# Squared-ReLU MLP by a seven-product scheme: operand differences made in the first product and kept in DRAM, the norm's factor moved to the second product's sums, the first two pairs of rows interleaved

## The chip, the cores and the metric

The kernel runs on one core of a Trainium2 chip. The metric is the device time of one execution in microseconds (us); lower is better. Of the core's engines, TensorE (PE in the profile) multiplies matrices, and its loading of the stationary operand is shown as PEld. VectorE (DVE), ScalarE (ACT) and GpSimd (POOL) work on tiles elementwise. SyncE (SP) issues most of the DMAs, in order. Each engine takes its own instructions in order, and semaphores join them.

## The reference

The trunk has two residual layers here: neighbourhood attention and an MLP, then a gated DeltaNet and an MLP, with a last norm behind them. SEQ and D_MODEL are 1024, D_FF is 4096, everything is float32. The change touches the two MLPs alone:

```python
def rmsnorm(x, w):
    y = xf * lax.rsqrt(jnp.mean(xf * xf, axis=-1, keepdims=True) + EPS)
    return (y * w.astype(jnp.float32)).astype(x.dtype)

def sq_relu_mlp(h, w1, w2):
    a = jax.nn.relu(h @ w1)
    return (a * a) @ w2

# in the trunk, for each layer:
x = x + mixer(rmsnorm(x, ...))
x = x + sq_relu_mlp(rmsnorm(x, mlp_norm[i]), mlp_w1[i], mlp_w2[i])
```

The mean of squares is one number per token. As the ReLU is taken of something that this positive number only scales, relu(r·u)² is r²·relu(u)², and r² may be multiplied in before or after the second product.

## The kernel before

Activations are kept transposed: 128 channels by 1024 tokens a tile, tokens in two halves of 512. A float32 product is made from a high and a low part of each operand, three matmuls for one (`hi·hi`, `hi·lo`, `lo·hi`). The high part is a copy by ScalarE (`whi` for weights, the left half of a tile for activations), the low part a subtraction by VectorE (`wlo`, the right half; line 242 in `halves`).

Both MLP products use a seven-product (Strassen-Winograd) scheme on 2 x 2 blocks: seven products in the order `ORDER = (1, 5, 2, 6, 3, 7, 4)` take the place of eight. Operands 5, 6, 7 and 4 are sums or differences of blocks. Four blocks of a right side are called 11, 12, 21, 22: the first digit is the even or odd tile of channels, the second the half of the tokens. One product is 12 matmuls of 128 x 512 (four tiles of the inner dimension, three matmuls each), and its result lies in one PSUM bank.

One MLP (`block`) runs in four stages.

1. `out_gather`: the mixer's output product is added to the residual stream `hs`; the sums of squares for the norm are made (`sumsq`), and the operands of the first product are prepared. Preparation that is late is left as functions in `todo`, called at the product that needs them.
2. `mlp_first` (matmuls at line 366): 16 pairs `n` of hidden tiles, seven products each. A pair loads its weights (`quad_weights`, 2 x 512 KB), makes four combinations of them on GpSimd (line 341), and finishes four results of 128 x 512: VectorE does ReLU and the multiplication by `rstd` in one instruction (line 346), ScalarE squares (line 347), and a DMA writes it to `hidden` in DRAM (line 348). In pair 0 the norm is finished between the first products: eight `ones` matmuls sum over the channels (line 194), GpSimd takes the power, eight matmuls spread the factor over the partitions (line 206).
3. `Second.blocks` (matmuls at line 1520): the first three quarters of the inner dimension of the second product, three blocks `b` of 28 products (seven positions, four output rows `q`). `load_b` reads the four blocks of `hidden`; GpSimd makes the four differences of them (`difference`), besides four combinations of weights (`combine`) and some of the sums, all through `less` (line 1359). `split` makes the high and low parts of the next position's operands; weights are split (lines 1513, 1514) in the step that uses them; the sums gather in `h`, `z`, `y`, `w`, of which `h` starts from the residual stream (line 1501).
4. `mlp_second` (matmuls at line 148, sums at line 409): the last quarter, plain, 16 tiles of 24 matmuls; each finished tile goes to `after` (the next norm, or `final_tile`).

The order in which instructions stand on an engine is made at compile time, outside the DeltaNet, by a scheduler that starts from the program's order and moves an instruction ahead where its own timing model says that it is ready. An engine's real order is therefore near the program's order, but not the same.

Of the kernel before, what the change touches and what calls it, by code (L numbers as in the profile page):

```python
# [37 lines left out]
class Trunk:  # L38
# [133 lines left out]
    def sumsq(self, d, half, hv, st):  # L172
        nc = self.nc
        if d == 0:
            st["acc", half] = self.half(f"rs{half}", 1)
# [13 lines left out]
    def rstd_cols(self, st, half, ps=None):  # L189
# [8 lines left out]
        return r  # L198

# [127 lines left out]
    def mlp_first(self, st, w1, get, spare, todo, second, moved):  # L327

        nc = self.nc
        self.hidden = self.dram.tile([w1.shape[1] // P, P, S], FP32, tag="hidden", name=self.uid("hidden"), bufs=1)  # L330
        nq = w1.shape[1] // (2 * P)
        raw = [self.quad_weights(w1, 0)]
        for n in range(nq):
            if n + 1 < nq:
                raw.append(self.quad_weights(w1, n + 1))
            a11, a12, a21, a22 = raw[n]
            own = {i: self.wk2.tile([P, 4, P], FP32, tag=f"s{i}", name=self.uid("s"), bufs=1)
                   for i in ((1, 2, 4, 3) if moved else (3, 1, 2, 4))}
            s1, s2, s3, s4 = [own[i] for i in range(1, 5)]
            for out, x, y, op in ((s1, a21, a22, ALU.add), (s2, s1, a11, ALU.subtract), (s4, a12, s2, ALU.subtract), (s3, a21, a11, ALU.subtract)):  # L340
                nc.gpsimd.tensor_tensor(out=out, in0=x, in1=y, op=op)
            left = {1: a11, 2: a12, 3: s4, 4: a22, 5: s1, 6: s2, 7: s3}
            temp = lambda i: self.slot(f"{spare}{i}", shape=[P, HALF])

            def finish(t, f, half):
                nc.vector.scalar_tensor_tensor(out=t, in0=t, scalar=0.0, in1=st["rstd", half], op0=ALU.max, op1=ALU.mult)  # L346
                nc.scalar.activation(out=t, in_=t, func=AF.Square)  # L347
                nc.sync.dma_start(out=self.hidden[2 * n + f][:, half * HALF:(half + 1) * HALF], in_=t)

            def add(out, x, y, eng=nc.vector):  # L350
                eng.tensor_tensor(out=out, in0=x, in1=y, op=ALU.add)  # L351
                return out

            for j in self.ORDER:
                hi, lo = [self.sb.tile([P, 4, P], F32R, tag=tag, name=self.uid(tag), bufs=3) for tag in ("whi", "wlo")]
                nc.scalar.copy(out=hi, in_=left[j])  # L356
                nc.vector.tensor_tensor(out=lo, in0=left[j], in1=hi.bitcast(FP32), op=ALU.subtract)  # L357
# [3 lines left out]
                pool, tag, bufs = {1: (self.pw, "p1", 1), 5: (self.pw, "p5", 1), 2: (self.ps, "mm", 2), 7: (self.ps, "mm", 2)}.get(j, (self.pw, "pq", 3))  # L361
# [5 lines left out]
                if n == 0 and j == 5:  # L367
                    rcol = [self.rstd_cols(st, half) for half in range(2)]
                if n == 0 and j == 2:
                    for half in range(2):  # L370
                        self.spread(st, half, rcol[half])
# [18 lines left out]
                second.prepare(n - nq, j)  # L390

    def mlp_second(self, a, h, w2, after, tail=2, cut=False):
        nc = self.nc
        w = [None, None]
        for d, half in self.sequence(tail):
            if w[0] != d:
                w = [d, self.weight(w2[w2.shape[0] - D:, d * P:(d + 1) * P])]
            hv = h(d, half)  # L400
            if cut and (d, half) == (ND - 1, 1):
                for part in range(2):
                    sl = slice(part * 256, part * 256 + 256)
                    ps = self.product(w[1], a, half, sl=slice(HALF + sl.start, HALF + sl.stop))
                    nc.vector.tensor_tensor(out=hv[:, sl], in0=ps, in1=hv[:, sl], op=ALU.add)
                    after(d, half, hv[:, sl], part)
                continue
# [908 lines left out]
class Second:  # L1316
# [6 lines left out]
    def __init__(self, tr, group, other, rest, free, w2):  # L1323
# [4 lines left out]
        self.names = {"11": free[4:6], "12": rest[0:2], "21": rest[2:4], "22": rest[4:5] + o(15)}  # L1328
        self.sets = g(0, 8, 1, 9), g(2, 10, 3, 11)
        self.acc = {"z": g(6, 7), "y": g(14, 15)}  # L1330
# [4 lines left out]
    def load_b(self, b, which, i):  # L1335

        nc, tr = self.tr.nc, self.tr
        t = tr.slot(self.names[which][i], shape=[P, 2, HALF])
        f, half = b * ND + 4 * i + int(which[0]) - 1, int(which[1]) - 1
        for k in range(2):  # L1340
            nc.sync.dma_start(out=t[:, k], in_=tr.hidden[f + 2 * k][:, half * HALF:(half + 1) * HALF])
            self.b[which, 2 * i + k] = t[:, k]
# [8 lines left out]
    def split(self, b, pos, i):  # L1351

        j = self.tr.ORDER[pos]
        t = self.tr.slot(self.sets[(7 * b + pos) % 2][i], F32R)
        self.tr.halves(t, self.b[{1: "11", 5: "11", 6: "11", 2: "21", 4: "21", 3: "22", 7: "12"}[j], i])
        self.ops[j, i] = t

    def less(self, out, x, y, op=ALU.subtract):
        self.tr.nc.gpsimd.tensor_tensor(out=out, in0=x, in1=y, op=op)  # L1359

    def difference(self, j, i):

        b = lambda which: self.b[which, i]
        if j == 5:
            self.less(b("11"), b("12"), b("11"))
        elif j == 6:
            self.less(b("11"), b("22"), b("11"))
        elif j == 7:
            self.less(b("12"), b("12"), b("22"))
        else:  # L1370
            self.less(b("21"), b("21"), b("11"))

    def left(self, j, q):
        if j in (5, 6):
            return self.s[q]
        t = self.k[self.block, 1 if j in (1, 7) else 2, q]
        return t[:, :, P:] if j in (7, 4) else t[:, :, :P]

    def combine(self, j, q):

        tr = self.tr
        if j == 5:
            self.s[q] = tr.work("s1", [P, 4, P], 4)
            self.less(self.s[q], self.left(7, q), self.left(4, q), ALU.add)
        elif j == 6:
            self.less(self.s[q], self.s[q], self.left(1, q))
        elif j == 7:
            self.less(self.left(7, q), self.left(7, q), self.left(1, q))
        else:
            self.less(self.left(2, q), self.left(2, q), self.s[q])  # L1390

    def prepare(self, n, j):
# [3 lines left out]
        if n == -3 and j in (1, 2):  # L1396
            self.load_b(0, "11", j - 1)
        if n < -1:
            return
        if j == 1:  # L1400
            for i in range(3):
                self.split(0, 0, i)
            self.load_b(0, "12", 0)
        elif j == 5:
            self.split(0, 0, 3)
            self.load_b(0, "12", 1)
        elif j == 2:
            for i in range(4):
                self.difference(5, i)
            self.load_b(0, "21", 0)  # L1410
            self.load_w(0, 1, 0)
        elif j == 6:
            self.load_b(0, "21", 1)
            for q in range(1, 4):
                self.load_w(0, 1, q)
        elif j == 3:
            for i in range(2):
                self.load_b(0, "22", i)

    def beside(self, b, pos, q):  # L1420

        last = b == self.nb - 1
        if pos < 6:
            self.split(b, pos + 1, q)
        elif not last:
            self.split(b + 1, 0, q)
        if pos == 0:
            self.combine(5, q)
        elif pos == 1:
            self.combine(6, q)  # L1430
            self.difference(6, q)
        elif pos == 2:
            self.difference(7, q)
        elif pos == 3:
            self.combine(3, q)
            self.difference(4, q)
        elif pos == 4:
            self.combine(7, q)
        if not last:
            if pos in (2, 3) and q % 2:  # L1440
                self.load_w(b + 1, 0, 2 * (pos - 2) + q // 2)
            elif pos == 4:
                self.load_b(b + 1, ("11", "22")[q // 2], q % 2)
            elif pos == 5 and q % 2:
                self.load_b(b + 1, "12", q // 2)
            elif pos == 6:
                self.difference(5, q)
                self.load_w(b + 1, 1, q)
                if q % 2:
                    self.load_b(b + 1, "21", q // 2)  # L1450
        else:
            n = 4 * pos + q
# [424 lines left out]
```

## Time and profile before

| what | value |
|---|---|
| median of 3 runs | 2818.93 us (2815.1 to 2823.02) |
| the profiled execution, its own time | 2822.13 us |
| its span, first to last instruction | 2820.3 us |
| mean granted TensorE clock | 0.977 |
| PE, DVE, ACT, POOL busy | 94%, 67%, 43%, 41% |
| DMA, mean | 92 GB/s |
| first MLP: first product, blocks, last quarter | from 605.8, 933.6, 1211.8 us |
| second MLP: first product, blocks, last quarter | from 2090.6, 2426.1, 2704.0 us |

Times in the trace are counted from the span's start. A row of a stretch gives the busy time of each engine and the number of its instructions in brackets, the granted clock as a share of full speed, and the DMA's share and rate. A row of a group gives a duration as least, median and greatest in ns. In a row of the timeline, the bracket at the end is the time that the engine sat idle before it, with what ended that.

### The profile page before, as it was taken

Reading aid. Unit: us, or ns where it says so; the run is one execution under the profiler, and the core shown is the slowest. Engines: PE = TensorE matmul, PEld = TensorE weight load, DVE = VectorE, ACT = ScalarE, POOL = GpSimd, SP = SyncE. Lnnn points to the kernel's source line nnn. Section 1 sums busy time; section 2 is a strip of 40 time slices with the busy share of each in tenths; the row PEclk is TensorE's granted clock in tenths of the full one; section 3 lists DMA queues with packets and bytes.
Section 4 is the critical chain, followed back from the end, with each engine's and each line's share of the span. In section 5 each row is a group of like instructions: output and inputs, shape, how many; then the busy total and the mean of one; then the engine's idle time right before and its main releaser. Section 6 shows DMA issues by size and latency. Waiting matters only on the chain. (4 is left out here: it accounts for less than half of the span.)

```text
span 2820.3 us, 40024 instructions
## 1 busy us (share of the span) xinstructions
PE 2662.4 (94%) x14172; PEld 2086.9 (74%) x14172; DVE 1883.8 (67%) x3381; ACT 1205.2 (43%) x2603; POOL 1169.1 (41%) x1207
## 2 busy tenths in 40 slices
PE   8999999999999889899999999999969999899898
PEld 6766666778888667687787877787858888677677
DVE  5155556665555878854778887887595555878853
ACT  5134444433334444333455555455353333444334
POOL 0111111154444764641344555543164444754741
PEclk9999999999999999999999999999979999999999
DMA  7212212343332623122221122214463332633023
GB/s 194 56 45 48 59 46 53 114 144 122 112 101 93 202 90 105 38 94 79 51 50 46 42 52 51 50 37 125 118 212 114 111 113 94 198 105 105 23 83 115
DMA packets 293430, 260.00 MB, mean 92 GB/s; under 512 B 78319, under 2 KB 230511, under 8 KB 293231
## 3 DMA queue, kind: packets, MB, share of 16 engines
q1 hardware_dynamic: 284814, 248.98, 29.6%
q0 software_dynamic: 3072, 8.39, 1.3%
q8 instruction: 111, 1.82, 0.3%
q10 hardware_dynamic: 5344, 0.09, 0.1%
q14 instruction: 89, 0.72, 0.1%
HBM read 182.52 MB, written 66.49 MB: 88 GB/s over the span
## 5 line engine op out<-in xcount | busy, mean ns | idle before, releaser
L1555 PE MATMUL mm<-A,whi 128*128 128x512 f32 x1216 | 406.2, 415 | 1.1 <-DVE A L1555 1.1
L148 PE MATMUL mm<-X,whi 128*128 128x512 f32 x1024 | 338.7, 403 | 0.7 <-ACT X L657 0.7
L1555 PEld LDWEIGHTS mm<-A,whi 128*128 128x128 f32 x1216 | 216.0, 192 | 41.4 <-DVE A L1555 1.9
L1555 PE MATMUL mm<-A,wlo 128*128 128x512 f32 x608 | 242.1, 398 | 0.0
L148 PEld LDWEIGHTS mm<-X,whi 128*128 128x128 f32 x1024 | 191.1, 189 | 47.4 <-issue 7.5
L148 PE MATMUL mm<-X,wlo 128*128 128x512 f32 x512 | 206.0, 403 | 0.0
L347 ACT ACTIVATE r<-r 128x512 f32<-128x512 f32 x128 | 80.9, 632 | 247.8 <-DVE r L346 245.1
L1555 POOL TENSOR_TENSOR xt<-lp,xi 128x126 f32<-128x126 f32 (+22 forms) x248 | 107.2, 432 | 175.4 <-DMA lp<-dsc 140.2
L357 DVE TENSOR_TENSOR wlo<-s,whi 128x512 fp32r<-128x512 f32 x128 | 121.7, 952 | 82.7 <-ACT whi L356 82.7
L180 POOL TENSOR_TENSOR rs<-rs,r 128x512 f32<-128x512 f32 x55 | 79.4, 1448 | 225.1 <-ACT r L179 225.0
L1555 DVE SCALAR_TENSOR_TENSOR X<-xp,cw,X 128x512 f32<-128x512 f32 x192 | 141.9, 780 | 1.8 <-ACT X L1555 1.1
L1555 PEld LDWEIGHTS mm<-A,wlo 128*128 128x128 f32 x608 | 115.8, 191 | 28.1
L242 DVE TENSOR_TENSOR X<-A,X 128x512 fp32r<-128x512 f32 x93 | 112.4, 1233 | 20.1 <-ACT X L241 19.5
L1555 POOL TENSOR_TENSOR xi<-xi,xt 128x126 f32<-128x126 f32 (+22 forms) x248 | 115.5, 466 | 19.4
L148 PE MATMUL mm<-A,whi 128*128 128x512 f32 (+1 forms) x336 | 109.8, 403 | 12.9 <-DVE hr L304 6.3
L1520 PE MATMUL pq<-X,whi 128*128 128x512 f32 x336 | 110.9, 412 | 10.6 <-ACT whi L1513 10.6
L1520 PE MATMUL pq<-A,whi 128*128 128x512 f32 x336 | 110.0, 409 | 11.5 <-ACT whi L1513 10.6
L598 POOL DMA_DIRECT2D wvraw<-qk x32 | 17.2, 539 | 248.1 <-ACT qk L596 241.5
L346 DVE SCALAR_TENSOR_TENSOR r<-r,rs 128x512 f32<-128x512 f32 x128 | 92.1, 720 | 37.6 <-POOL r L351 37.6
L242 DVE TENSOR_TENSOR A<-X,A 128x512 fp32r<-128x512 f32 x84 | 101.7, 1235 | 20.2 <-ACT A L241 19.6
L128 ACT CAST whi<-wraw 128x512 fp32r<-128x512 f32 (+1 forms) x110 | 66.1, 605 | 108.6 <-PE mm L148 58.2
L148 PEld LDWEIGHTS mm<-X,wlo 128*128 128x128 f32 x512 | 96.6, 189 | 20.8 <-issue 1.7
(396 smaller groups left out, 7245.9 us busy)
## 6 DMA issues: line engine op xcount, KB each, us to landing
quad<-in_mlp_w_dram SPq DMA_DIRECT2D x64, 512.0 KB
hidden<-r SPq DMA_DIRECT2D x128, 256.0 KB
wraw<-in_gdn_w_in_dram SPq DMA_DIRECT2D x64, 256.0 KB
wraw<-in_mlp_w_dram SPq DMA_DIRECT2D x52, 256.0 KB
X<-in_mlp_w_dram SPq DMA_DIRECT2D x24, 512.0 KB
X<-hidden SPq DMA_DIRECT2D x48, 256.0 KB
A<-in_mlp_w_dram SPq DMA_DIRECT2D x24, 512.0 KB
A<-hidden SPq DMA_DIRECT2D x48, 256.0 KB
```

Of the source, the lines that this page charges most:

```text
L128: nc.scalar.copy(out=hi[:, :nk], in_=raw[:, :nk])
L148: nc.tensor.matmul(out=ps, lhsT=a, rhs=b[:, sl], start=n == 0, stop=n == last)
L180: nc.gpsimd.tensor_tensor(out=st["acc", half], in0=st["acc", half], in1=sq, op=ALU.add)
L242: nc.vector.tensor_tensor(out=t[:, HALF:], in0=src, in1=t[:, :HALF].bitcast(FP32), op=ALU.subtract)
L346: nc.vector.scalar_tensor_tensor(out=t, in0=t, scalar=0.0, in1=st["rstd", half], op0=ALU.max, op1=ALU.mult)
L347: nc.scalar.activation(out=t, in_=t, func=AF.Square)
L357: nc.vector.tensor_tensor(out=lo, in0=left[j], in1=hi.bitcast(FP32), op=ALU.subtract)
L598: nc.gpsimd.dma_start(out=ks[i][ab[1 - i], sl].bitcast(FP32), in_=khi[ab[i], sl].bitcast(FP32))
L1520: nc.tensor.matmul(out=ps, lhsT=u[:, i], rhs=x[:, v:v + HALF], start=i == 0 and n == 0, stop=i == 3 and n == 2)
L1555: r = f(*args, **kw)
```

## The change

- In `mlp_first`, ReLU is done by ScalarE without `rstd`; the norm's sums and its spread are no longer made there.
- The four differences of the finished blocks that the second product needs are made there too, on VectorE (`less`), for the first 12 of 16 pairs, and written to a new DRAM tensor `diff`. GpSimd's two additions of a pair become one, VectorE's five from PSUM become six.
- Pairs 0 and 1 take turns for their first four products; pair 0's weight combinations lie in other buffers, `first`.
- In `Second`, an operand set is loaded ready from `hidden` or `diff`, two positions ahead (`load_b`, seven sets of four tiles in a block where there were four); `difference` is gone. Weights are split two products ahead (`split_w`). The residual stream isn't the start of the sums any more, and the copy `r` of product 1 with its addition to `z` is gone.
- `norm_squares` in the middle of the blocks (product 42 of 84) makes 1/(mean of squares) with VectorE's reciprocal and spreads it. In `mlp_second` each tile gets two more VectorE instructions: times this factor, plus the residual stream, which is loaded one tile ahead (`fetch`).
- The sums of squares of the following norm lie in other buffers (`st["at"]`), as the old ones live longer.

```diff
-                self.mlp_first(st, w1, get, other, todo, second, moved)
+                self.mlp_first(w1, get, other, (free[-1], free[0]), todo, second)
...
-            a, h = second.blocks()
-            self.mlp_second(a, h, w2, after, **how)
+            self.mlp_second(second.blocks(st), second.sums, st, w2, after, **how)
...
+    def norm_squares(self, st):
+        nc = self.nc
+        ps = self.bank("pa", [P, HALF])
+        for j in range(8):
+            nc.tensor.matmul(out=ps[:, j:j + 1], lhsT=st["acc", j // 4][:, j % 4 * P:(j % 4 + 1) * P], rhs=self.ones[:, 0:1],
+                             start=True, stop=True)
+        r = self.sb.tile([P, 8], FP32, tag="rcol8", name=self.uid("rcol"), bufs=1)
+        nc.vector.tensor_scalar(out=r, in0=ps[:, 0:8], scalar1=1.0 / D, scalar2=EPS, op0=ALU.mult, op1=ALU.add)
+        nc.vector.reciprocal(out=r, in_=r)
+        for half in range(2):
+            self.spread(st, half, r[:, 4 * half:4 * half + 4])
...
             def finish(t, f, half):
-                nc.vector.scalar_tensor_tensor(out=t, in0=t, scalar=0.0, in1=st["rstd", half], op0=ALU.max, op1=ALU.mult)
+                nc.scalar.activation(out=t, in_=t, func=AF.Relu)
                 nc.scalar.activation(out=t, in_=t, func=AF.Square)
                 nc.sync.dma_start(out=self.hidden[2 * n + f][:, half * HALF:(half + 1) * HALF], in_=t)
+                return t
+
+            def less(i, out, x, y):
+                if n < nq - 4:
+                    nc.vector.tensor_tensor(out=out, in0=x, in1=y, op=ALU.subtract)
+                    nc.sync.dma_start(out=self.diff[n, i], in_=out)
...
                 elif j == 2:
-                    finish(add(self.half("r2"), ps, p1), 0, 0)
+                    c11 = finish(add(result("r2"), ps, p1), 0, 0)
                 elif j == 6:
                     u2 = add(temp(15), ps, p1)
+                    nc.gpsimd.tensor_tensor(out=p5, in0=p5, in1=u2, op=ALU.add)
                 elif j == 3:
-                    t = add(self.half("r"), ps, p5)
-                    finish(add(t, t, u2, nc.gpsimd), 0, 1)
+                    c12 = finish(add(result("r"), ps, p5), 0, 1)
+                    less(0, c11, c12, c11)
                 elif j == 7:
                     add(p1, ps, u2)
-                    finish(add(self.half("r"), p5, p1, nc.gpsimd), 1, 1)
+                    c22 = finish(add(p5 if n == 1 else self.half("r"), ps, p5), 1, 1)
+                    less(1, u2, c22, c11)
+                    less(2, c12, c12, c22)
                 else:
-                    finish(add(self.half("r2"), ps, p1), 1, 0)
+                    c21 = finish(add(result("r2"), ps, p1), 1, 0)
+                    less(3, c11, c21, u2)
...
+        quads, shared, s = [quad(n) for n in range(nq)], {}, {}
+        for n in (0, 1) + (0, 1) * 5 + (0,) * 3 + (2,) + (1,) * 3:
+            next(quads[n], None)
...
     (mlp_second)
-            ps = self.product(w[1], a, half)
-            nc.vector.tensor_tensor(out=hv, in0=ps, in1=hv, op=ALU.add)
-            after(d, half, hv)
+            fetch(n + 1)
...
+                hv = sums[d, half][:, sl]
+                nc.vector.tensor_tensor(out=hv, in0=ps, in1=hv, op=ALU.add)
+                nc.vector.tensor_tensor(out=hv, in0=hv, in1=st["rstd", half][:, sl], op=ALU.mult)
+                nc.vector.tensor_tensor(out=hv, in0=hv, in1=hs[d, half][:, sl], op=ALU.add)
...
     (Second)
-    def load_b(self, b, which, i):
+    def load_b(self, s, k):
...
+        t = tr.slot(self.raw[s % 2][k], shape=[P, 2, HALF])
+        j = tr.ORDER[s % 7]
+        for i in range(2):
+            pair = s // 7 * 4 + 2 * k + i
+            if j < 4:
+                src = tr.hidden[2 * pair + (j > 1)][:, (j > 2) * HALF:(1 + (j > 2)) * HALF]
+            else:
+                src = tr.diff[pair, (5, 6, 7, 4).index(j)]
+            nc.sync.dma_start(out=t[:, i], in_=src)
+            self.b[s, 2 * k + i] = t[:, i]
...
     (beside)
+        s = 7 * b + pos
+        self.split(s + 1, q)
+        if q < 2:
+            self.load_b(s + 2, q)
+        if pos in (0, 1, 3, 4):
+            self.combine(b, (5, 6, 0, 3, 7)[pos], q)
...
     (blocks)
+        for m in range(2):
+            self.split_w(m)
+        for m in range(28 * self.nb):
+            b, pos, q = m // 28, m // 4 % 7, m % 4
+            j = tr.ORDER[pos]
+            self.split_w(m + 2)
...
+            if b:
+                nc.vector.tensor_tensor(out=out, in0=ps, in1=out, op=ALU.add)
+            else:
+                nc.scalar.copy(out=out, in_=ps)
+            self.beside(b, pos, q)
+            if m == 42:
+                tr.norm_squares(st)
```

More of the change, by code (lines that the diff above doesn't have):

```diff
@@ L325, in quad_weights, with mlp_first @@
         return out[0][:, :, :P], out[1][:, :, :P], out[0][:, :, P:], out[1][:, :, P:]
-    def mlp_first(self, st, w1, get, spare, todo, second, moved):
+    def mlp_first(self, w1, get, spare, first, todo, second):
         nc = self.nc
         self.hidden = self.dram.tile([w1.shape[1] // P, P, S], FP32, tag="hidden", name=self.uid("hidden"), bufs=1)
+        self.diff = self.dram.tile([w1.shape[1] // P - ND, 4, P, HALF], FP32, tag="diff", name=self.uid("diff"), bufs=1)
         nq = w1.shape[1] // (2 * P)
[L332 to L335, printed above, removed]
-            a11, a12, a21, a22 = raw[n]
[L337 to L343, printed above, removed]
@@ new lines, in quad, with temp, result @@
+        def quad(n):
+            load(n)
+            yield
+            a11, a12, a21, a22 = raw[n]
+            if n < 2:
+                for i in (1, 2, 4, 3):
+                    combine(n, i)
+            def temp(i):
+                if n < 2:
+                    if i not in shared:
+                        shared[i] = self.slot(f"{spare}{i}", shape=[P, 2, HALF])
+                    return shared[i][:, n]
+                return self.slot(f"{spare}{i}", shape=[P, HALF])
+            def result(tag):
+                return self.wraw().rearrange("p a c -> p (a c)") if n == 1 else self.half(tag)
@@ new lines, in mlp_first, with mlp_second, fetch @@
+        for n in range(2, nq):
+            for i, _ in enumerate(quads[n]):
+                if i == 0 and n + 1 < nq:
+                    next(quads[n + 1])
+    def mlp_second(self, a, sums, st, w2, after, tail=2, cut=False):
+        nc = self.nc
+        w, hs, seq = [None, None], {}, self.sequence(tail)
+        old = self.hs
+        def fetch(n):
+            if n < len(seq):
+                d, half = seq[n]
+                hs[d, half] = t = self.work("hr", [P, HALF], 2)
+                nc.sync.dma_start(out=t, in_=old[d][:, half * HALF:(half + 1) * HALF])
+        fetch(0)
+        for n, (d, half) in enumerate(seq):
@@ L398, in mlp_second @@
             if w[0] != d:
                 w = [d, self.weight(w2[w2.shape[0] - D:, d * P:(d + 1) * P])]
[L400 to L407, printed above, removed]
@@ L408, in mlp_second @@
-            ps = self.product(w[1], a, half)
-            nc.vector.tensor_tensor(out=hv, in0=ps, in1=hv, op=ALU.add)
-            after(d, half, hv)
+            fetch(n + 1)
+            for part in range(2) if cut and n == len(seq) - 1 else (None,):
+                sl = slice(0, HALF) if part is None else slice(part * 256, part * 256 + 256)
+                ps = self.product(w[1], a, half, sl=slice(half * HALF + sl.start, half * HALF + sl.stop))
+                hv = sums[d, half][:, sl]
+                nc.vector.tensor_tensor(out=hv, in0=ps, in1=hv, op=ALU.add)
+                nc.vector.tensor_tensor(out=hv, in0=hv, in1=st["rstd", half][:, sl], op=ALU.mult)
+                nc.vector.tensor_tensor(out=hv, in0=hv, in1=hs[d, half][:, sl], op=ALU.add)
+                after(d, half, hv, *(() if part is None else (part,)))
@@ L1333, in __init__ @@
         self.ready = []
-    def load_b(self, b, which, i):
+    def load_b(self, s, k):
         nc, tr = self.tr.nc, self.tr
[L1338 to L1342, printed above, removed]
+        if s >= 7 * self.nb:
+            return
+        t = tr.slot(self.raw[s % 2][k], shape=[P, 2, HALF])
[8 more added lines that the diff above has]
+            self.b[s, 2 * k + i] = t[:, i]
     def load_w(self, b, k, q):
@@ L1485, in whole, with blocks @@
         self.n = len(self.ready)
-    def blocks(self):
+    def blocks(self, st):
         tr, nc = self.tr, self.tr.nc
-        self.h, self.sums = {}, {}
-        for which in "zyw":
+        self.sums, self.w = {}, {}
+        for which in "rqyw":
             for i in range(2):
```

236 lines of the change are left out of this document (95 added, 141 removed).

## The prediction

> **What bounds the kernel now.** The page's busy table, read first, names TensorE.
>
> ```profile
> PE 2662.4 (94%) x14172; PEld 2086.9 (74%) x14172; DVE 1883.8 (67%) x3381; ACT 1205.2 (43%) x2603; POOL 1169.1 (41%) x1207
> ```
>
> A share over the whole span hides stages, so I cut the span at the first matmuls of each stage and read busy time by stretch. The columns are the length, then PE, PEld, DVE, ACT and POOL busy, each with its count, then the granted clock, the DMA share and GB/s.
>
> ```profile
> 605.80:933.60 327.80, 321.49 (x1377) 257.80 (x1376) 196.27 (x270) 129.28 (x225) 155.10 (x106) 0.98 0.37 117
> 650.00:900.00 250.00, 250.00 (x1077) 201.12 (x1076) 144.23 (x204) 95.77 (x167) 113.59 (x77) 1.00 0.34 110
> 933.60:1211.80 278.20, 249.00 (x1009) 192.48 (x1010) 232.58 (x247) 111.34 (x191) 178.68 (x113) 0.96 0.30 97
> 2090.60:2426.10 335.50, 323.84 (x1377) 259.92 (x1375) 203.97 (x280) 130.22 (x227) 159.68 (x108) 0.97 0.37 118
> 2426.10:2704.00 277.90, 248.75 (x1008) 192.50 (x1009) 234.71 (x247) 111.19 (x191) 178.13 (x113) 0.96 0.30 97
> 2704.00:2811.10 107.10, 101.45 (x489) 82.06 (x487) 41.70 (x84) 45.96 (x96) 36.24 (x28) 0.97 0.32 96
> ```
>
> The second row is the middle of a first product: TensorE never stops, and 250 us hold 1077 matmuls, 0.2321 us each. That is the yardstick. The blocks of one MLP are 84 products of 12 matmuls, 1008 × 0.2321 = 234.0 us, and take 278.2 and 277.9: 44.2 and 43.9 too long, 88.1 together. A first product is 1344 matmuls, 312.0 us, and takes 327.8 and 335.5: 15.8 and 23.5 too long. These four numbers, 127.4 us, are what there is to win, apart from the last stage.
>
> Next, who keeps TensorE waiting in the blocks, and how the blocks look in pieces.
>
> ```profile
>   DVE wlo L1514: 36.2, 38
>   ACT whi L1513: 25.1, 6
> 960.00:1026.00 66.00, 63.74 (x270) 50.53 (x271) 55.27 (x61) 28.93 (x50) 35.08 (x22) 1.00 0.42 134
> 1026.00:1060.00 34.00, 25.61 (x96) 18.90 (x95) 25.54 (x24) 11.95 (x22) 33.84 (x23) 0.85 0.00 1
> 1060.00:1110.00 50.00, 48.13 (x206) 38.22 (x205) 42.13 (x56) 21.39 (x35) 13.79 (x9) 1.00 0.42 135
> 1110.00:1160.00 50.00, 41.27 (x154) 31.37 (x152) 42.61 (x38) 15.93 (x28) 49.77 (x32) 0.86 0.05 14
> 933.60:1211.80 278.20, 177.90 (x112) 0.96 0.30 97
> ```
>
> The named culprit is the split of the weights, by VectorE and ScalarE. But the four pieces show whom these wait for: where GpSimd is busy without a gap (33.84 of 34, 49.77 of 50), TensorE did 96 and 154 matmuls, 22.3 and 35.7 us of work, and lost 26.0 of 84 us. Where GpSimd is half busy or less it did 270 and 206, 62.7 and 47.8 us, and lost 5.5 of 116. The last row counts GpSimd's line 1359 alone: 112 instructions, 177.9 us, 1.588 us each. Beside them VectorE itself is slow:
>
> ```profile
> L242 DVE TENSOR_TENSOR A<-X,A 128x512 fp32r<-128x512 f32 x76 | 95.0, 1276 | 16.6 <-ACT A L241 16.3
> L1514 DVE TENSOR_TENSOR wlo<-s,whi 128x512 fp32r<-128x512 f32 x24 | 26.1, 1089 | 0.0
> L242 DVE TENSOR_TENSOR A<-X,A x84: 677/1337/1827, 914.4 to 1193.9; 128x512 fp32r<-128x512 f32 x84
> L1501 DVE TENSOR_TENSOR h<-pq,h x48: 676/679/693, 946.5 to 2701.4; 128x512 f32<-128x512 f32 x48
> ```
>
> The same subtraction of SBUF tiles takes 0.68 to 1.83 us, while the addition that reads PSUM always takes 0.68.
>
> **The change, part by part.** *Blocks.* GpSimd loses, for one MLP, 48 differences, and its 32 additions become 28; 48 combinations stay: 76 × 1.588 = 120.7 us in some 245, 49% busy. That lies between the two calm pieces (35.08 of 66 is 53%, 13.79 of 50 is 28%), so they are the nearest rows: 5.5 us lost on 110.5 of work is 5.0%, and 5.0% of 234.0 is 11.7 us. A count of VectorE agrees. A product needs one addition, one weight split and one activation split: 0.68 + 1.09 + 1.28 = 3.05 us at the means of today, 0.27 more than TensorE's 2.785; that overload stands only where GpSimd makes combinations, 16 products of 28, so 3 × 16 × 0.265 = 12.7 us. The bounds: with all splits at 0.68 a product needs 2.04 us and nothing is lost; with the weight split at its mean and the other at its greatest, 0.68 + 1.09 + 1.83 = 3.60 us, it is 3 × 16 × 0.815 = 39.1, nearly as bad as now. I take 11.7. ScalarE has two splits of 0.62 and in block 0 a copy, under 2 us of 2.785. The loads grow from 16 to 28 of 256 KB a block, 3 MB in some 80 us on top of 97 GB/s, about 135 GB/s, a rate that 1060 to 1110 already has.
>
> *The norm* moves into the blocks with 16 tiny matmuls. What they cost on a busy TensorE is seen in the DeltaNet, and what they cost today at the start of the first MLP:
>
> ```profile
> 1304.07 0.95 PE L1555 MATMUL pa<-ones,rs 128*128 128x1 f32 x8
> 1307.06 1.06 PE L1555 MATMUL pa<-ident,rcol 128*128 128x128 f32 x8
> 608.90 1.05 PE L194 MATMUL pa<-ones,rs 128*128 128x1 f32 x8
> 618.95 1.22 PE L366 MATMUL p<-A,whi 128*128 128x512 f32 x2 [1.19 <-ACT whi L356]
> 2099.71 1.87 PE L194 MATMUL pa<-ones,rs 128*128 128x1 f32 x8 [5.39 <-POOL rs L180]
> 607.68 12.71 SPq L323 DMA_DIRECT2D quad<-in_mlp_w_dram  x3
> 2105.52 5.47 SPq L323 DMA_DIRECT2D quad<-in_mlp_w_dram  x3
> qk<-r POOLq DMA_DIRECT2D x32, 128.0 KB, 2.3
> ```
>
> A row is one half's sums or spread, so both halves take 2 × 0.95 + 2 × 1.06 = 4.0 us; a wait for VectorE's reciprocal is bounded by 0 and by the 1.19 us above, and I take 0, since product 43 can go ahead. Blocks: 234.0 + 11.7 + 4.0 = 249.7 us instead of 278.2 and 277.9, a gain of 28.5 + 28.2 = 56.7.
>
> *Start of the first product.* From 608.9 to 618.95 TensorE does hardly anything but the norm, and in the second MLP it waits 5.39 us for GpSimd's sum; both go, and so, I take it, does the short stop before the blocks, as the first weights there are split ahead. What is late next is pair 1's weights, as its first product is now second in the program. Their DMAs stand in SP's queue behind a buffer that `out_gather` must leave: issued from 607.7 and from 2105.5. TensorE is through with its first product at 608.6 and 2093.4. Counting 4 us from issue to use (the 128 KB store of the last row took 2.3 to land), the wait is 3 us in the first MLP. In the second it is 0 if other products of pair 0 go ahead, 16 if the order is kept; nothing in the trace decides, and I take the middle, 8. A wait costs more than itself: the blocks waited 36.2 + 25.1 us and lost 88.1, 1.42 to one, and here is why:
>
> ```profile
> 1122.71 0.50 PE L1520 MATMUL pq<-A,wlo 128*128 128x512 f32 x1 [2.20 <-DVE wlo L1514]
> 1123.05 0.63 PE L1520 MATMUL pq<-A,whi 128*128 128x512 f32 x2
> 1124.72 1.05 PE L1520 MATMUL pq<-A,whi 128*128 128x512 f32 x2
> ```
>
> After a wait of 2.20 us the pair of matmuls goes from 0.63 to 1.05 us. So 3 and 8 become 4.3 and 11.4, where 15.8 and 23.5 stand now: a gain of 11.5 + 12.1 = 23.6, bounds 0 and 39.3. The Trainium skill ("TensorE: Matmul & The Clock Gate", on the HAM clock gate and in its closing table) says that the clock halves after an idle window of about 3.4 us and asks for no gaps over about 3 us. By that rule the 3 us wait costs only itself and the gain would be 1.3 us more; the trace has the slow clock behind 2.20 us, and the measurement decides.
>
> *Rest of the first product.* VectorE: a pair loses four multiplications and gains an addition from PSUM and four differences; ScalarE gains four ReLUs; GpSimd loses one addition.
>
> ```profile
> L346 DVE SCALAR_TENSOR_TENSOR r<-r,rs x128: 677/685/1782, 627.8 to 2432.0; 128x512 f32<-128x512 f32 x128
> L347 ACT ACTIVATE r<-r x128: 630/632/637, 628.5 to 2433.8; 128x512 f32<-128x512 f32 x128
> L1555 ACT ACT_TABLE_LOAD x21 | 26.9, 1283 | 0.4
> ```
>
> A pair lasts 84 × 0.2321 = 19.5 us. VectorE has 144.23/250 of it, 11.2, less 4 × 0.68, plus 0.68, plus four of 0.68 to 1.83: 11.9 to 16.5. ScalarE has 95.77/250, 7.5, and gets 4 × 0.632: 10.0. TensorE stays the cover, so I cost all this at nothing; without that cover it would be up to 5 × 0.68 = 3.4 us for each of 24 pairs. The four stores more go through SP's queue; a buffer of `r2` must be stored before it is written again 8.3 us (three products) after the last product, and the chain to the store (0.68 + 0.63 + 0.63 + 0.68) with 2.3 to 4.6 us for 256 KB ends at 4.9 to 7.2, inside.
>
> *Last quarter.* Two more instructions of VectorE for each of 32 tiles lie inside 5.6 us of matmuls. At the very end two of 256 elements are bare, 2 × 0.42 = 0.8 us from the nearest row, line 405's addition:
>
> ```profile
> L405 DVE TENSOR_TENSOR w<-mm,w x2: 416/419/422, 2807.4 to 2811.1; 128x256 f32<-128x256 f32 x2
> 2711.24 0.32 SPq L1469 DMA_DIRECT2D h<-hs  x1
> 2714.97 0.62 ACT L128 CAST whi<-wraw 128x512 fp32r<-128x512 f32 x1 [5.64 <-DMA wraw<-in_mlp_w_dram]
> 2716.79 1.11 PE L433 MATMUL tr<-ident,r 128*128 128x128 f32 x4 [4.68 <-ACT r L430]
> ```
>
> There ScalarE sat behind a weight DMA, which SP had issued behind a load of the residual into a busy buffer; TensorE lost 4.68 us, by 1.42 to one 6.6. That load is gone, but the new `fetch` can stop the same queue for the same reason. Between 0 and 6.6 I take 4.
>
> *Sum.* −56.7 − 23.6 − 4 + 0.8 = −83.5 us. The profiled execution took 2822.1 by its own time, so 2738.6; it stands 3.2 us above the median of the runs, so I predict **2735 us**.
>
> **Rivals.** *VectorE beside GpSimd stays the bound.* At 3.60 us a product the blocks lose 39.1 + 4.0 = 43.1, 1.9 us less than now in both MLPs, and only the start and the end gain: 2819 − 1.9 − 23.6 − 4 + 0.8 = 2790. For it: VectorE was busy 232.58 of 278.20. Against: these durations belong to pieces with GpSimd full, and it sheds a third.
>
> *Table loads for the new ReLU.* No ReLU is in the trace. If it and the square each needed a table load of 1.283 us, a pair had eight, ScalarE 10.0 + 10.3 = 20.3 us of 19.5, 0.8 over in 32 pairs: 26 us, 2761. Against: copies and squares alternate in this stage without a load. The Trainium skill ("ScalarE: Activation LUTs", on table sets) puts ReLU and copy in every set, so that no load would come.
>
> *Slower: the round trip through DRAM.* An operand set now waits for its own load; a buffer pair is loaded again only when its last set is split, and ScalarE's next instructions queue behind a late one.
>
> ```profile
> ACT X L1483 <- DMA X<-hidden: 25.2, 7, 6.3
> ```
>
> At this row's 3.6 us a wait, 42 sets cost 151 us, and the time is 2735 + 151 = 2886. It decides from 83.5/42 = 2.0 us a set. Against: there are four products, 11 us, between issue and use.
>
> *It doesn't do what it says:* the split moved ahead by two products still stands behind other work in VectorE's queue, and new waits equal the old: 2819.
>
> **How the numbers follow.** Forecast (2693 to 2765, its own range): 0.70, the table case within it. VectorE bound, 2765 to 2810: 0.18. No change: 0.04. Slower: 0.08. The low end is all of the excess but the norm, 88.1 − 8.0 + 39.3 + 6.6 = 126 below the median, 2693. The high end takes in most of the second case: 2787. Faster by over 0.3%, about what a measurement can tell from no change here, is 0.88, same 0.04, slower 0.08.
>
> **What would show it.** Blocks of 246 to 253 us each with GpSimd near half busy, and waits for `wlo` under 10 us an MLP; activation splits with a mean near 1.0 us or below; first products of 316 and 323 us without norm matmuls at line 366's start, but with a wait for pair 1's weights; no ACT_TABLE_LOAD there. I am wrong if ScalarE's splits wait for `diff` or `hidden`, if TensorE stops in the middle of a first product, or if VectorE fills the blocks.

## Result and profile after

The changed kernel takes **2749.16 us** (median of 4 runs, 2746.52 to 2750.87) against 2819.43 us (median of 4) for the kernel before: a ratio of 0.9751, with a 95% interval of 0.9734 to 0.9768. 2735 was predicted.

The busy table of its page stands first. TensorE has the same 14172 matmuls; VectorE and GpSimd are relieved, ScalarE got 91 us more.

```profile
span 2748.6 us, 40384 instructions
PE 2631.3 (96%) x14172; PEld 2076.3 (76%) x14172; DVE 1845.1 (67%) x3407; ACT 1296.2 (47%) x2747; POOL 941.5 (34%) x1067
```

Next comes the span cut at the first matmuls of each stage, with the columns of the table before: length, then PE, PEld, DVE, ACT, POOL busy, granted clock, DMA share, GB/s. The first three rows are the first MLP's first product, the middle of it, and the blocks; the last three are the second MLP's first product, blocks and last quarter.

```profile
607.00:930.60 323.60, 315.38 (x1345) 253.64 (x1344) 197.66 (x271) 168.98 (x287) 122.95 (x85) 0.99 0.49 160
650.00:900.00 250.00, 249.69 (x1073) 201.52 (x1072) 150.26 (x213) 129.63 (x220) 92.27 (x65) 1.00 0.49 162
930.60:1173.80 243.20, 240.71 (x1042) 192.90 (x1041) 186.37 (x226) 117.85 (x202) 100.07 (x65) 1.00 0.43 139
2052.80:2390.30 337.50, 316.56 (x1346) 254.36 (x1345) 208.40 (x281) 170.52 (x291) 126.54 (x87) 0.96 0.48 156
2390.30:2634.40 244.10, 240.77 (x1042) 192.81 (x1041) 185.30 (x226) 117.48 (x202) 100.35 (x66) 1.00 0.42 138
2634.40:2738.40 104.00, 99.60 (x489) 80.18 (x487) 66.38 (x115) 45.66 (x96) 32.03 (x24) 1.00 0.42 127
```

Against the rows of before, the difference of the two spans, 71.7 us, splits like this (us):

| stage | before | after | difference | forecast |
|---|---|---|---|---|
| blocks, first MLP | 278.2 | 243.2 | −35.0 | −28.5 |
| blocks, second MLP | 277.9 | 244.1 | −33.8 | −28.2 |
| first product, first MLP | 327.8 | 323.6 | −4.2 | −11.5 |
| first product, second MLP | 335.5 | 337.5 | +2.0 | −12.1 |
| last quarter, second MLP | 107.1 | 104.0 | −3.1 | −4 |
| tail | 9.2 | 10.2 | +1.0 | +0.8 |
| all else | | | +1.4 | 0 |

So nearly all of the gain, 68.8 us, comes from the blocks, and the first product, where 23.6 us were expected, gives 2.2. Three rows from the list of what TensorE waited for (total, times, longest), and the matmuls on both sides of the longest wait, show both.

```profile
PE pq L415 <- ACT whi L404: 28.0, 2, 20.5
PE mm L1557 <- DVE wlo L1462: 3.0, 5, 0.9
PE pq L1557 <- DVE wlo L1462: 2.5, 5, 0.7
```

```profile
617.47 1.22 PE L415 MATMUL pq<-A,whi 128*128 128x512 f32 x2 [7.46 <-ACT whi L404]
2055.47 0.39 PE L415 MATMUL p<-A,wlo 128*128 128x512 f32 x1
2076.39 1.22 PE L415 MATMUL pq<-X,whi 128*128 128x512 f32 x2 [20.53 <-ACT whi L404]
2078.30 1.05 PE L415 MATMUL pq<-X,whi 128*128 128x512 f32 x2
2082.14 0.69 PE L415 MATMUL p<-X,whi 128*128 128x512 f32 x2
```

In the blocks the 61.3 us of waits (36.2 + 25.1) have become 5.5. The waits at line 415 are new: pair 0 has made one product, and the next in the order is pair 1's. Rows of VectorE, SP and ScalarE in the same timeline say why it is late:

```profile
2063.22 1.75 DVE L257 SCALAR_TENSOR_TENSOR A<-hr,g_m,A 128x512 fp32r<-128x512 f32 x1
2066.81 2.18 SPq L1422 DMA_DIRECT2D A<-in_mlp_w_dram  x2
2069.14 0.94 SPq L335 DMA_DIRECT2D quad<-in_mlp_w_dram  x2
2075.72 0.62 ACT L404 CAST whi<-quad 128x512 fp32r<-128x512 f32 x1 [8.98 <-DMA quad<-in_mlp_w_dram]
2076.25 0.61 ACT L404 CAST whi<-A 128x512 fp32r<-128x512 f32 x1
```

Pair 1's weights go into a buffer that shares its place with `hr` of `out_gather`, whose last reader ends at 2064.97 (first row). SP first issues two loads for the blocks (line 1422), which the scheduler had moved ahead, then pair 1's at 2069.14; they are split from 2075.72. The split of `A`, pair 0's next product, stands behind them in ScalarE's queue, so pair 0 can't go ahead either.

### The profile page after: what moved, and what is told of

It reads as the page before. It is cut to its first block, busy times and chain, and to the rows that moved or that the text cites. A ratio compares the mean times of both kernels' runs of the same rounds, so it can differ in the third digit from the quotient of the medians.

```text
span 2748.6 us, 40384 instructions
## 1 busy us (share of the span) xinstructions
PE 2631.3 (96%) x14172; PEld 2076.3 (76%) x14172; DVE 1845.1 (67%) x3407; ACT 1296.2 (47%) x2747; POOL 941.5 (34%) x1067
## 5 line engine op out<-in xcount | busy, mean ns | idle before, releaser
L1581 PE MATMUL mm<-A,whi 128*128 128x512 f32 x1216 | 404.6, 414 | 1.1 <-DVE A L1581 1.1
L147 PE MATMUL mm<-X,whi 128*128 128x512 f32 x1024 | 339.7, 404 | 0.7 <-ACT X L723 0.7
L405 DVE TENSOR_TENSOR wlo<-s,whi 128x512 fp32r<-128x512 f32 x120 | 99.5, 830 | 41.6 <-ACT whi L404 41.3
L415 PE MATMUL pq<-X,whi 128*128 128x512 f32 x304 | 97.0, 401 | 20.5 <-ACT whi L404 20.5
L128 DVE TENSOR_TENSOR wlo<-wraw,whi 128x512 fp32r<-128x512 f32 (+1 forms) x110 | 95.2, 869 | 25.5 <-ACT whi L127 24.7
L404 ACT CAST whi<-s 128x512 fp32r<-128x512 f32 x120 | 74.3, 619 | 78.6 <-PE mm L415 51.9
L1557 PE MATMUL mm<-A,whi 128*128 128x512 f32 x336 | 106.0, 396 | 0.0
L1557 PE MATMUL mm<-X,whi 128*128 128x512 f32 x336 | 105.9, 396 | 0.0
L1557 PE MATMUL pq<-X,whi 128*128 128x512 f32 x336 | 105.8, 396 | 0.0
```

Source lines behind the costliest of these rows:

```text
L128: nc.vector.tensor_tensor(out=lo[:, :nk], in0=raw[:, :nk], in1=hi[:, :nk].bitcast(FP32), op=ALU.subtract)
L147: nc.tensor.matmul(out=ps, lhsT=a, rhs=b[:, sl], start=n == 0, stop=n == last)
L404: nc.scalar.copy(out=hi, in_=left)
L405: nc.vector.tensor_tensor(out=lo, in0=left, in1=hi.bitcast(FP32), op=ALU.subtract)
L415: nc.tensor.matmul(out=ps, lhsT=u[:, i], rhs=x[:, v:v + HALF], start=i == 0 and m == 0, stop=i == 3 and m == 2)
L1557: nc.tensor.matmul(out=ps, lhsT=u[:, i], rhs=x[:, v:v + HALF], start=i == 0 and n == 0, stop=i == 3 and n == 2)
```

## Experiments

Theories on the gain: C, GpSimd's relief makes VectorE fast and so the blocks; D, the weight splits two products ahead make it. On the loss at the start: A, the turns make TensorE wait for pair 1's weights. Four kernels came first (the kernel before: 2818.82 us beside them).

**seq_pairs**: pair 0 is finished before pair 1 begins.

```diff
-        for n in (0, 1) + (0, 1) * 5 + (0,) * 3 + (2,) + (1,) * 3:
+        for n in (0, 1) + (0,) * 8 + (2,) + (1,) * 8:
```

> The changed kernel, with pair 0 finished before pair 1 begins (both pairs' weights are still asked for at the start). Theory A, the turns cost the start: TensorE stood 7.46 and 20.53 us for pair 1's weights, with slow-clock matmuls behind each; with pair 0 going on, its operands are ready from some 2060 us of the trace and pair 1's weights at 2075.7, so most of that goes, 20 to 30 us: 2719 to 2729. Rival B, the turns are needed: pair 0's late operands, made by VectorE beside GpSimd, take the place of the weights as the wait: 2740 to 2760.

Measured: **2735.99 us** (2732.49 to 2737.62), ratio 0.9706 (0.9691 to 0.972), so 13 us faster than the changed kernel and the fastest of all that ran. The first products take 317.2 and 330.0 us. A holds in sign, but of the 20 to 30 us that it expected 13 came: with all of pair 0's products in a row TensorE now waits for VectorE, busy with late operands, as rival B said. Three of the waits in the second MLP:

```profile
2047.35 0.50 PE L415 MATMUL p<-X,wlo 128*128 128x512 f32 x1 [1.28 <-DVE wlo L405]
2047.69 0.62 PE L415 MATMUL p<-X,whi 128*128 128x512 f32 x2
2054.10 0.51 PE L415 MATMUL p<-X,wlo 128*128 128x512 f32 x1 [3.23 <-DVE wlo L405]
2054.44 1.03 PE L415 MATMUL p<-X,whi 128*128 128x512 f32 x2
2060.86 0.50 PE L415 MATMUL mm<-X,wlo 128*128 128x512 f32 x1 [2.00 <-DVE wlo L405]
2061.20 0.97 PE L415 MATMUL mm<-X,whi 128*128 128x512 f32 x2
```

**no_ahead** (the changed kernel, weights split in their own step) and **ahead_only** (the kernel before, weights split two products ahead, the same edit the other way round):

```diff
-        for m in range(2):
-            self.split_w(m)
...
-            self.split_w(m + 2)
+            self.split_w(m)
```

> The changed kernel, with the weights of the blocks split in the step that uses them instead of two products ahead. Theory C, GpSimd's relief makes the gain: the blocks keep most of it, 245 to 255 us each instead of 243.2 and 244.1, time 2752 to 2770. Rival D, the order of the weight splits makes the gain: waits for the splits return, blocks of 265 us and more, 2790 or above.

> The kernel before, with only the blocks' weight splits two products ahead; nothing else of the change. Theory C: GpSimd is still full, so the blocks stay at 268 to 278 us, 2800 to 2820. Rival D: the waits for the splits (61.3 us in the kernel before) go, blocks of 250 us or less, 2750 to 2765.

Measured: 2750.17 us, ratio 0.9757 (0.9743 to 0.9772), and 2821.27 us, ratio 1.0008 (0.9998 to 1.0017). The lookahead is worth nothing in either kernel. D falls.

**pool_load**: the changed kernel with 48 subtractions per MLP on GpSimd, on a tile that nobody else uses, at the positions where the differences stood.

```diff
+        if pos in (1, 2, 3, 6):
+            self.add(self.idle, self.idle, self.idle, ALU.subtract)
...
```

> The changed kernel, with 48 subtractions of 128x512 added on GpSimd in the blocks of each MLP, at the positions where the differences were, on a private tile that nothing else reads or writes. They do no work for the output. Theory C, GpSimd's load is the cause: 76 us of GpSimd work come back, VectorE's splits get longer, combinations late, blocks of 260 to 278 us, 2780 to 2815. Rival D, order is the cause: blocks within 5 us of 243, 2749 to 2760.

Measured: 2793.94 us, ratio 0.9915 (0.9898 to 0.9931). Nobody reads the results of these subtractions, and still 44.8 of the 70 us are gone; the blocks take 264.6 and 265.7. Groups of VectorE in the first MLP's blocks (busy, mean ns of one), first of the changed kernel, then of pool_load, and last two stretches of pool_load, the whole of these blocks and a part:

```profile
L254 DVE TENSOR_TENSOR A<-X,A 128x512 fp32r<-128x512 f32 x76 | 73.4, 991 | 3.4 <-ACT A L253 3.1
L1462 DVE TENSOR_TENSOR wlo<-s,whi 128x512 fp32r<-128x512 f32 x24 | 20.1, 837 | 7.3 <-ACT whi L1461 7.3
L1560 DVE TENSOR_TENSOR c<-pq,c 128x512 f32<-128x512 f32 x12 | 8.2, 682 | 3.2 <-PE pq L1557 3.2
```

```profile
L254 DVE TENSOR_TENSOR A<-X,A 128x512 fp32r<-128x512 f32 x76 | 90.7, 1222 | 1.6 <-ACT A L253 1.1
L1462 DVE TENSOR_TENSOR wlo<-s,whi 128x512 fp32r<-128x512 f32 x24 | 27.0, 1129 | 7.1 <-ACT whi L1461 7.1
L1564 DVE TENSOR_TENSOR c<-pq,c 128x512 f32<-128x512 f32 x12 | 8.2, 683 | 2.7 <-PE pq L1561 2.7
```

```profile
929.90:1194.50 264.60, 248.14 (x1042) 194.44 (x1041) 215.15 (x226) 117.61 (x202) 161.16 (x113) 0.97 0.38 127
972.00:1006.00 34.00, 22.68 (x72) 15.66 (x71) 13.93 (x13) 10.27 (x20) 32.68 (x27) 0.80 0.16 52
```

The same 226 VectorE instructions take 215 us instead of 186, and of the groups shown only those with two SBUF inputs grew; the addition that reads PSUM stays at 0.68. The Trainium skill ("SBUF — State Buffer", on who interferes with whom) states this: a VectorE instruction with two SBUF inputs contends with a GpSimd instruction that reads SBUF, one with at most one does not. The trace agrees, 991 to 1222 ns against 682 to 683.

So GpSimd's load alone can cost 21.4 and 21.6 us of the blocks' 35.0 and 33.8. But C's way, slow VectorE, is not how most of it is lost. The last row is 34 us with 72 matmuls, 16.7 us of work: 17.3 of the 21.4 us are lost there, with VectorE busy for 13.93 us only (in the second MLP 36.0 us hold 75 matmuls, 18.6 us lost). Rows of GpSimd, ScalarE and TensorE show why:

```profile
967.60 9.51 POOL L1433 TENSOR_TENSOR idle<-idle 128x512 f32<-128x512 f32 x7
977.07 1.26 POOL L1433 TENSOR_TENSOR s<-s,X 128x512 f32<-128x512 f32 x1
978.37 0.62 ACT L1461 CAST whi<-s 128x512 fp32r<-128x512 f32 x1 [9.06 <-POOL s L1433]
979.04 1.22 PE L1561 MATMUL mm<-A,whi 128*128 128x512 f32 x2 [3.86 <-ACT whi L1461]
```

A combination of weights (second row) stands in GpSimd's queue behind seven added subtractions; its split on ScalarE waits 9.06 us for it, and TensorE waits in turn. TensorE's waits for `whi`, none in the changed kernel's blocks, are 10.7 us in these blocks, those for `wlo` 5.6. What is shown is a late queue on GpSimd; that slower VectorE instructions cost TensorE much is not shown by this run.

Where is the rest? The first guess was the path: in the kernel before, the splits wait for the differences.

**pool_path**: 44 subtractions of zero per MLP, each between an operand's load and its split, two products ahead of the split.

```diff
+        at, i = (s + 2, q - 2) if q > 1 else (s + 1, q + 2)
+        if 1 < at < 7 * self.nb and tr.ORDER[at % 7] > 3:
+            self.add(self.b[at, i], self.b[at, i], self.idle, ALU.subtract)
...
```

> The changed kernel, with 44 subtractions of a zero tile per MLP put back on GpSimd, each on a loaded difference between its load and its activation split (two products ahead of the split): the results stay the same. As many GpSimd instructions as in pool_load, less four, but now the splits wait for them. If GpSimd's load alone explains what pool_load gave back, it comes out as pool_load did less a twelfth, 2790 us, with blocks of 263 to 265 us. If the rest of the blocks' gain (24 us of 68.8) came from taking GpSimd out of the path from hidden to split, it comes to 2810 to 2818, with blocks of 275 to 278.

Measured: 2779.77 us, ratio 0.9859 (0.9842 to 0.9875): less than either theory, though GpSimd and VectorE are as busy as before the change (176 and 227 us, blocks of 257.6). The path falls as the cause, and the busy times of two engines do not fix the loss: it matters at which products GpSimd's work stands, and what stands behind it.

A look back at the trace of before gives another candidate, ScalarE's queue. Its timeline at one place, with rows of ScalarE, VectorE and TensorE, and the group of the copies (busy, mean ns, idle time before them):

```profile
1137.24 0.59 ACT L1535 COPY r<-pq 128x512 f32<-128x512 f32 x1 [8.94 <-POOL A L1359]
1137.72 1.14 ACT L241 CAST A<-X 128x512 fp32r<-128x512 f32 x2
1138.38 1.83 DVE L242 TENSOR_TENSOR A<-X,A 128x512 fp32r<-128x512 f32 x1 [7.25 <-ACT A L241]
1138.76 0.62 ACT L1513 CAST whi<-s 128x512 fp32r<-128x512 f32 x1
1139.43 1.22 PE L1520 MATMUL pq<-A,whi 128*128 128x512 f32 x2 [4.18 <-ACT whi L1513]
```

```profile
L1535 ACT COPY r<-pq 128x512 f32<-128x512 f32 x4 | 2.3, 586 | 24.2 <-POOL A L1359 19.1 <-DVE h L1501 5.1
```

The copy of product 1's sum to `r` waits 8.94 us for GpSimd to give `r` back, and ScalarE's splits, VectorE's behind them and TensorE wait with it. The change removed that copy. Theory E: the copy in front of a full GpSimd is the rest.

**no_copy**: the kernel before with that one edit. **path_copy** and **copy_only**: pool_path and the changed kernel with the copy put back.

```diff
     (no_copy)
-                            r = tr.half("r")
-                            nc.scalar.copy(out=r, in_=ps)
-                            self.less(z, z, r, ALU.add)
+                            add(z, ps)
     (path_copy, copy_only)
+            if b and j == 1:
+                r = tr.half("r")
+                nc.scalar.copy(out=r, in_=ps)
+                self.add(out, r)
...
```

> The kernel before, with one edit: from block 1 on the first product's sum goes to z by VectorE's addition from PSUM; before, ScalarE copied it to a buffer r and GpSimd added r to z. Eight copies of ScalarE and eight additions of GpSimd fewer per MLP, eight additions of VectorE (0.68 us) more; nothing else of the change. In the trace of before the third of these copies of a block waits 10.17 and 8.94 us for GpSimd to give r back, ScalarE's splits stand behind it, and TensorE waits 10.6 us per MLP for them. If that queue is the part of the blocks' gain that GpSimd's load does not explain, the blocks fall from 278 to 260 to 266 us each, and the time to 2783 to 2795. If GpSimd is late whatever stands in its queue, only its eight additions are saved, at pool_load's 0.45 us for each one 3.6 us per MLP: 2812, and a wait for another of its results stands where the copy's stood.

> pool_path (the changed kernel with 44 subtractions of zero per MLP on GpSimd, between load and split; 2779.8 us) with the copies put back: from block 1 on ScalarE copies the first product's sum to r and GpSimd adds it. If ScalarE's queue behind that copy is the rest of the blocks' gain, the time goes back to 2800 to 2815, with blocks of 268 to 276 us and waits of ScalarE for GpSimd before the copy. If only the load counts, eight additions more at 0.45 us make it 2787, blocks of 261 to 263.

> The changed kernel with only the copies put back, and GpSimd without other work added. If the copy hurts only where GpSimd is full, r comes back in time, and it is 2749 to 2756 us with blocks of 243 to 247. If the round trip over GpSimd is by itself too long for the two buffers r, it is 2765 to 2775, with blocks of 251 to 256.

Measured: no_copy 2790.98 us, ratio 0.99 (0.9883 to 0.9916), blocks of 264.9 and 265.2; path_copy 2792.23, ratio 0.9906 (0.9891 to 0.9921), blocks of 266.5 and 265.0; copy_only 2755.96, ratio 0.9773 (0.9759 to 0.9788), blocks of 245.0 and 246.6. One edit of three lines takes 13.3 and 12.7 us off the blocks, as theory E expected and more than its rival allows, and TensorE's waits for `whi` at line 1520 fall from 25.1 us to 4.0 (second fence). path_copy lies between the two expectations: put back beside pool_path, the copies wait less for GpSimd (4.0 and 6.2 us for the two banks in the first MLP's blocks, against 19.1 for one) and cost less. What the copy costs depends on how full GpSimd is: 2 us an MLP where GpSimd is relieved, 6 to 9 beside pool_path's load (6 by the medians; path_copy's profiled execution took 5.4 us more than its median), 13 in the kernel before. no_copy also takes eight additions from GpSimd and gives them to VectorE, whose busy time went up, from 232.6 to 236.2 us (its stretch of the first MLP's blocks). What TensorE still waits for there is `wlo`, 37.8 us in both MLPs:

```profile
932.30:1197.20 264.90, 243.56 (x1009) 188.54 (x1010) 236.17 (x255) 107.98 (x183) 171.36 (x105) 0.99 0.31 102
```

```profile
PE pq L1520 <- DVE wlo L1514: 24.6, 20, 2.6
PE mm L1520 <- DVE wlo L1514: 13.2, 22, 2.0
PE mm L1520 <- ACT whi L1513: 4.0, 2, 2.0
```

**no_copy_ahead** and **path_copy_late** ask whether the lookahead counts once the copy is away, or in path_copy. Both edits are shown above.

> The kernel before with two edits: no_copy's (the first product's sum goes to z by VectorE, 2791.0 us alone) and ahead_only's (weight splits two products ahead, 2821.3 us alone, no gain). The differences stay on GpSimd. If the lookahead was worth nothing only because ScalarE's queue stood behind the copy, it now takes part of the waits for wlo that no_copy still has (37.8 us in both MLPs), and the blocks come to 254 to 260 us, near pool_path's 257.6 and 258.9: 2770 to 2780. If VectorE's slow splits are too long for any order, it stays at 2788 to 2793.

> path_copy (the changed kernel with 44 subtractions per MLP on GpSimd and the copies put back, 2792.2 us) without the lookahead: weight splits stand in their own product again. What then remains of the change in the blocks is that each operand set has its own loads, the 28 instead of 32 additions and the norm's matmuls. If these three together are the blocks' gain, the blocks go back to 274 to 279 us and the time to 2808 to 2820. If the lookahead is worth nothing here too, as in no_ahead, it stays at 2790 to 2796, and the rest lies in the own loads, which end the chain over one buffer that three products' operands share.

Measured: 2792.64 us, ratio 0.9909 (0.9894 to 0.9924), and 2789.91 us, ratio 0.9898 (0.9881 to 0.9914). Nothing again, in four kernels.

For the start, **after_queue** keeps the blocks' first loads behind pair 1's in SP's queue, and **lag4** lets pair 0 make four products before the turns begin.

```diff
     (after_queue, load_w)
+        with tr.tc.issue_after(tr.q1.ins) if (b, k) == (0, 0) else nullcontext():
             nc.sync.dma_start(out=t, in_=src[k])
...
     (lag4)
-        for n in (0, 1) + (0, 1) * 5 + (0,) * 3 + (2,) + (1,) * 3:
+        for n in (0, 1) + (0,) * 5 + (1,) + (1, 0) * 3 + (2,) + (1,) * 4:
```

> The changed kernel with one order of issue fixed: the four loads of the blocks' first weights, which SP issued at 2051.38 and 2066.81 ahead of pair 1's weights, go behind them in SP's queue. If SP's queue adds to the wait of 20.5 us for pair 1's weights, these are issued when their buffer comes free, at about 2065 instead of 2069, and the second MLP's first product falls from 337.5 to 332 to 334 us, the first MLP's stays at 323.6: 2744 us. If only the buffer that out_gather holds sets the time, or the bandwidth at that place, nothing changes: 2749.

> The changed kernel with the turns begun later: pair 0 makes four products alone, then the two pairs take turns, then pair 1 makes its last four. It lies between the changed kernel (first products of 323.6 and 337.5 us) and seq_pairs (317.2 and 330.0). If the start loses the smaller of two things, the wait for pair 1's weights and the pace of VectorE's splits for pair 0, it beats both: 315 and 328, 2733 us. If VectorE's pace is lost in any order that begins with pair 0 alone, it is seq_pairs with part of the wait for the weights on top in the second MLP: 318 and 333, 2740 us.

Measured: after_queue 2746.67 us, ratio 0.974 (0.9725 to 0.9754); its second first product takes 331.5 us, 6.0 less, as its weights are issued at 2065.98, as soon as the buffer is free:

```profile
2065.98 0.94 SPq L335 DMA_DIRECT2D quad<-in_mlp_w_dram  x2
2071.21 1.22 PE L417 MATMUL pq<-X,whi 128*128 128x512 f32 x2 [14.35 <-ACT whi L406]
```

So of the 20.5 us some 6 are what stood in front on SP, and 14 the shared buffer and the transfer itself. The medians differ by only 2.5 us, and the intervals overlap; the stage shows the effect, the time hardly. lag4 takes 2742.13 us, ratio 0.9725 (0.971 to 0.9739), with first products of 319.2 and 330.0: between the two orders in the first MLP, level with seq_pairs in the second, and better than both in neither. Its stretch from the end of the first MLP's blocks to the second's `out_gather` is 5.6 us longer than in the changed kernel (841.1 against 835.5), which no theory here explains; the profiled execution took 3.1 us more than its median.

## Why the prediction was right, and where not

The forecast was the likeliest case, its own range (2693 to 2765) holds the time, and the sign and the place are right: the blocks. But two of its terms were off by some 12 and 21 us in opposite directions, and one cause was left out. That the total came within 14 us is in part luck.

- **Blocks, −56.7 forecast, −68.8 measured.** The mis-sized term is the 11.7 us of loss that remained in each MLP. It was taken from two stretches of before with GpSimd half busy (5.5 us lost on 110.5 of work), and a count with VectorE's durations of before (1.28 and 1.09 us) agreed. With GpSimd relieved the durations fell to 0.99 and 0.84, and 5.5 and 6.4 us of loss remained beside the norm's matmuls; VectorE is busy 186 of 243 us, and waits of 5.5 us are left in both MLPs together. The yardstick, 0.2321 us a matmul, held within 0.4%.
- **The cause is half shown and half argued.** The prediction put the whole loss of the blocks down to GpSimd slowing VectorE, and costed the copy's removal at nothing, though its wait of 19.1 us was in the trace. By no_copy the copy to `r` in ScalarE's queue is 13.3 and 12.7 us. For the rest, 21.7 and 21.1 us between no_copy and the changed kernel, the traces fit the prediction: in no_copy TensorE waits for `wlo`, VectorE is busy 236.2 of 264.9 us, and in the changed kernel both shrink together with the durations of the splits. But no run changes VectorE's durations by themselves, nor gives the operand sets their own loads without the rest, so this half stays argued. pool_load doesn't prove it: its 21.4 and 21.6 us are mostly late combinations, and that they make up the measured 35.0 and 33.8 together with no_copy's is luck. The costs do not add in every order either: path_copy has load and copy, and stands 12 us an MLP short of before. Whether that is the positions of GpSimd's work or the buffers shared by three operand sets, no run here settles.
- **Start of the first product, −23.6 forecast, −2.2 measured.** This step failed. The wait in the second MLP, put at the middle of 0 and 16, was 20.53: the order was kept, since ScalarE's queue holds pair 0's next split behind pair 1's, and the end of the bound was short too, because two loads stood in front on SP and the weights needed 7.2 us from issue (2069.14) to use (2076.39) where 4 were counted. In the first MLP it was 7.46 instead of 3. The waits that were to go did go.
- **A wait costs 1.42 times itself** lies between what came: the first product is 11.6 us over 312.0 behind a wait of 7.46, 1.55 to one, and 25.5 behind 20.53, 1.24 to one. What came on top of the wait is 4.1 and 5.0 us: in these two rows nearer to a fixed price than to a share.
- **The norm's matmuls** take 1.8 + 1.9 us in the blocks, against 4.0 forecast, and nothing waits for the reciprocal:

```profile
L204 PE MATMUL pa<-ones,rs 128*128 128x1 f32 x16 | 1.8, 245 | 0.0
L218 PE MATMUL pa<-ident,rcol 128*128 128x128 f32 x16 | 1.9, 275 | 0.0
L385 ACT ACTIVATE r<-r 128x512 f32<-128x512 f32 x120 | 76.0, 633 | 116.2 <-DVE r L397 113.5
L1581 ACT ACT_TABLE_LOAD x21 | 26.9, 1283 | 0.4
```

- **ReLU on ScalarE** (third row) is free under TensorE: 0.633 us each and no table load with it. The 21 loads in the whole trace are the DeltaNet's, as before.
- **Last quarter**, −4 of 0 to 6.6 forecast, −3.1 measured: the longest wait there fell from 4.68 to 2.3 us:

```profile
PE tr L499 <- ACT r L496: 2.5, 2, 2.3
```

- **Rivals.** "VectorE stays the bound" (2790) did not come. pool_load's 2794 is near that figure by another way, late combinations. Of "it doesn't do what it says" one part came, the lookahead is worth nothing in four kernels, but the waits went all the same. The round trip through DRAM costs the blocks nothing visible: TensorE's waits in them are for `wlo` alone.

## What to carry to other kernels

An engine that is 41% busy over the span, as GpSimd was, can still set the pace of a stage. Two ways are shown here: a buffer that it returns late stops an in-order queue with everything behind (no_copy), and work that nobody needs soon, ahead in its own queue, makes late what others wait for (pool_load). A third is seen, its price not isolated: another engine's two-input instructions are longer beside it. Look for the first in the idle column of the small instructions (four copies of 2.3 us in all had 24.2 us of idle before them), not among the costly groups. And where work is interleaved to spread a load, ask when the second stream's data can be there at all: it stands in the same queues as the first.

## What the runs showed of the hardware

- The slow clock can come behind waits as short as 2 us, but not behind every one: in seq_pairs a pair of matmuls takes 0.62 us behind a wait of 1.28 us, 0.97 and 1.03 behind waits of 2.00 and 3.23, and yet 0.63 behind one of 3.13 (below). The length of a wait alone does not decide it. Behind 20.53 us it is back at nearly full speed 5.8 us later (2082.14). The Trainium skill ("TensorE: Matmul & The Clock Gate", on the HAM clock gate) puts the limit at an idle window of some 3.4 us; the rows with 2.00 and 3.23 show it below that.

```profile
636.08 0.50 PE L415 MATMUL mm<-A,wlo 128*128 128x512 f32 x1 [3.13 <-DVE wlo L405]
636.42 0.63 PE L415 MATMUL mm<-A,whi 128*128 128x512 f32 x2
```

- In the middle of a first product TensorE has hardly a gap (249.69 of 250 us busy), and yet 250 us hold 1073 matmuls instead of 1077, while the DMA rate is 162 GB/s instead of 110 and ScalarE is busier. That is 0.4%, 1.2 us in a first product. The 0.31 us of gaps are worth one of the four; what does the rest was not tried.
